# Making the low parts of fetched operands with an accumulating transfer

## The chip, the cores and the metric

The kernel runs on one core of a Trainium2 chip. The metric is the device time of one execution in microseconds (us). The engines of a core are named as in the profile: PE is TensorE (matrix products), with PEld for its weight loads; DVE is VectorE and ACT is ScalarE; POOL is GpSimd, and SP is SyncE, which here only issues transfers.

## The reference

One inference step of a transformer layer of width 2048, in fp32, over 512 prompt frames and 8 × 16 new frames, 640 tokens in all. Two groups of attention heads share one input projection; then come the output projection, a gated feed-forward block of 44 × 128 = 5632 columns and a last norm. The change touches the feed-forward block alone:

```python
def merge_and_ffn(x, oa, ob, norm_grp_a, norm_grp_b, w_out, norm_ffn, w_gate, w_up, w_down):
    o = jnp.concatenate([rmsnorm(oa, norm_grp_a), rmsnorm(ob, norm_grp_b)], axis=-1)
    x = x + o @ w_out
    h = rmsnorm(x, norm_ffn)
    return x + (jax.nn.silu(h @ w_gate) * (h @ w_up)) @ w_down
...
    y_prompt = rmsnorm(xp, norm_final)
```

## The kernel before, in words

**Two parts of a number.** An fp32 value goes to PE as a high part, rounded to the format fp32r, and a low part, the value minus the high part. `split` makes both: ACT writes the high part (L168), DVE subtracts it from the value (L169). `mm3` then issues three matmuls per tile: high weight by high operand (L177), high weight by low operand (L178), low weight by high operand (L179).

**Seven products for eight.** Matrices are cut into 2 × 2 blocks, and the four output blocks are built from seven products instead of eight. The tokens are cut into two halves of HT = 320. `quartet` loads four blocks of a weight matrix with SP (L874), forms sums of them on DVE (L887, L889) and on POOL (L891, which overwrites b11 and is needed by p5; L898, which overwrites b21 and is needed by p4), and multiplies in the order p1, p6, p7, p2, p5, p4, p3. Each product is emptied from its bank on ACT or DVE (L908). The operand sums that belong to product number `which` (0 to 6) are prepared once.

**Half 1** loops over 22 pairs of column blocks, for each over w_gate and w_up, K = 8 tiles per product. The gate goes through a Silu and two multiplications (L970 to L972), the product of gate and up is made on DVE (L976), and POOL forms the four operand sums that half 2 needs (L980 to L983). Three blocks of the pair as they are and the four sums, seven tiles in all, are stored by SP to `act_d` in DRAM, in four transfers (L984, and L986 three times).

**Half 2** walks 32 steps t. Step t adds to output blocks t mod 8 and t mod 8 + 8 the products over the five or six pairs that are active then (the table START says when a pair enters; it stays for eight steps). A pair's seven operands come back from `act_d` by `fetch`: SP loads a raw tile of 128 x 320 (L918), ACT writes its high part (L920), and DVE (where `which` is a multiple of 3) or POOL subtracts to give the low part (L921). The fetches for pairs that enter at step t + 1 are issued two products after the one that frees their space, in `fetch_waiting`. Blocks of x2 that a step adds to are loaded at L1010 and L1011. From step 24 on, squares of the finished blocks are also summed, on POOL (L248).

**The transition** is the last w_up quartet of half 1. As each of its products ends, `free(which)` releases the operands of half 1 and fetches those of the five pairs of step 0: pair loads of two tiles (L932), then `fetch` on each, the low part of the first of two on DVE and of the second on POOL. That makes 35 fetches, and the steps do 154 more.

**Order.** Each engine takes its instructions from one queue in order. The framework that builds the kernel lays the queues, so that the order on an engine isn't everywhere that of the text; it also adds the semaphore waits.

Of the kernel before, what the change touches and what calls it, by code (L numbers as in the profile page):

```python
# [7 lines left out]
AF = mybir.ActivationFunctionType  # L8
ALU = mybir.AluOpType
# [8 lines left out]
HT = 320  # L18
# [10 lines left out]
NPAIR = NFF // 2  # L29
# [4 lines left out]
def active(step):  # L34

    return [j for j in range(NPAIR) if (step - START[j]) % STEPS < 8]
# [5 lines left out]
def f(ap):  # L42
    return ap.bitcast(F32)


def halves(ap):
    return ap.rearrange("p (a b) -> p a b", a=2)


class Net:  # L50
# [20 lines left out]
    def add(self, queue, work):  # L71
        self.queues.setdefault(queue, []).append(work)
# [179 lines left out]
def sh(t, *shape):  # L252
    v = t[:, :int(np.prod(shape))]
    if len(shape) == 2:
        v = v.rearrange("p (a b) -> p a b", a=shape[0])
    elif len(shape) == 3:
        v = v.rearrange("p (a b c) -> p a b c", a=shape[0], b=shape[1])
    return v
# [11 lines left out]
def build(nc, tc, io, pools):  # L270
    n = Net(nc, tc, io, pools)
    dma = nc.sync.dma_start
# [12 lines left out]
    def dram(name, shape):  # L285
        return pools["dr"].tile(list(shape), F32, tag=name, name=name)
# [7 lines left out]
    def pack(t, k):  # L294
        v = r(sh(t, 2, k))
        return v[:, 0], v[:, 1]
# [476 lines left out]
    x2_d, act_d = dram("x2_d", (KT, P, TOK)), dram("act_d", (7, P, NPAIR, HT))  # L773
# [135 lines left out]
    prep = prepare([5, 6, 7], [7])  # L909
    lefts = [[None] * 7 for _ in range(NPAIR)]  # L910

    def fetch(j, which, raw=None, engine=nc.gpsimd):
        t, spare = n.get("S"), None
        if raw is None:
            if len(n.lists["S"]) > 3:
                spare = n.get("S")
            raw = n.scratch() if spare is None else spare[:, :HT]
            dma(out=raw, in_=act_d[which, :, j])  # L918
        hi, lo = hl = pack(t, HT)
        nc.scalar.activation(hi, raw, AF.Identity)  # L920
        engine.tensor_tensor(lo, raw, f(hi), ALU.subtract)  # L921
        if spare is not None:
            n.put("S", spare)
        lefts[j][which] = t, hl

    def free(which):
        n.put("S", *(h[which][0] for h in hs))
        ready = active(0)
        for j in ready[::2]:
            k = min(2, ready[-1] + 1 - j)  # L930
            raw = n.get("S")
            dma(out=sh(raw, k, HT), in_=act_d[which, :, j:j + k])  # L932
            for a in range(k):
                fetch(j + a, which, raw[:, a * HT:a * HT + HT], (nc.vector, nc.gpsimd)[a])
            n.put("S", raw)

    gate = None
    for i in range(NPAIR):
        for src in ("w_gate", "w_up"):
            blocks = [(2 * i, 0), (2 * i + 1, 0), (2 * i, 8), (2 * i + 1, 8)]  # L940
            load = lambda z: io[src][blocks[z][0], :, blocks[z][1]:blocks[z][1] + 8]
            y = n.get("S"), n.get("S")
            c11, c21, c12, c22 = y[0][:, :HT], y[0][:, HT:], y[1][:, :HT], y[1][:, HT:]
            start, end = i == 0 and src == "w_gate", i == NPAIR - 1 and src == "w_up"
            for step, bank in quartet(8, load, hs, (lambda w: next(prep)) if start else None, free if end else None):
                if step == "p1":
                    nc.scalar.activation(c11, bank, AF.Identity)
                elif step == "p6":
                    add(c12, c11, bank)
                elif step == "p7":  # L950
                    add(c21, c12, bank)
                elif step == "p5":
                    add(c22, c21, bank)
                    add(c12, c12, bank)
                elif step == "p2":
                    add(c11, c11, bank)
                elif step == "p4":
                    add(c21, c21, bank)
                elif step == "p3":
                    add(c12, c12, bank)  # L960
            if start:
                for _ in prep:
                    pass
                n.move("W", "H", 2)
                r_f = n.get("S")
                n.rstd(ssq, D, r_f)
                n.put("S", ssq)
            if src == "w_gate":
                for x in y:
                    nc.vector.tensor_tensor(x, x, r_f, ALU.mult)  # L970
                    nc.scalar.activation(x, x, AF.Silu)
                    nc.gpsimd.tensor_tensor(x, x, r_f, ALU.mult)  # L972
                gate = y
            else:
                for x, g in zip(y, gate):
                    nc.vector.tensor_tensor(x, x, g, ALU.mult)  # L976
                u, w = gate
                tt = nc.gpsimd.tensor_tensor
                s3, s1, s2, s4 = u[:, :HT], u[:, HT:], w[:, :HT], w[:, HT:]
                tt(s1, c21, c22, ALU.add)  # L980
                tt(s3, c21, c11, ALU.subtract)
                tt(s2, s1, c11, ALU.subtract)
                tt(s4, c12, s2, ALU.subtract)  # L983
                dma(out=act_d[0, :, i], in_=c11)  # L984
                for t, pick in ((w, slice(1, 7, 5)), (u, slice(2, 4)), (y[1], slice(4, 6))):
                    dma(out=act_d[pick, :, i].rearrange("w p c -> p w c"), in_=halves(t))  # L986
                n.put("S", *gate, *y)
    n.put("S", r_f)

# [3 lines left out]
    def fetch_waiting(left):  # L993
        while len(waiting) > left:
            for j, which in waiting.pop(0):
                fetch(j, which, engine=(nc.vector if which % 3 == 0 else nc.gpsimd))

    def step(t, part="all"):
        now = active(t)
# [3 lines left out]
        def after(which):  # L1003
            n.put("S", *(lefts[j][which][0] for j in now if j not in nxt))
            waiting.append([(j, which) for j in nxt if j not in now])
            fetch_waiting(2)
# [79 lines left out]
    for name in step(STEPS - 2, "late"):  # L1086
        if name == "p2":
            next(norm)
    fetch_waiting(0)
    squares(6, 0)  # L1090
    pass
# [98 lines left out]
```

## Time and profile before

| what | value |
|---|---|
| median of 3 runs | 2677.78 us (2677.6 to 2683.37) |
| the profiled execution | 2685.62 us, span 2683.8 us, mean granted clock 0.989 |
| PE, DVE, ACT, POOL busy | 2600.3, 1925.1, 1081.2, 789.5 us |
| bytes moved by transfers | 332.23 MB, mean 124 GB/s |
| half 1 ends, half 2 begins | about 2068 us into the span |

Busy time is that of an engine's compute instructions. SP's rows, marked SPq, are issues of transfers and their waits. A row of a timeline gives the start in us, the duration in us, engine, line, operation, the output's and inputs' names and the tile; in brackets stand the idle time before it and what ended it. In groups by line the columns are busy us and mean ns, then the idle time before and what ended it; in the table of waits: us in total, times, longest. W are weight tiles, S operand and sum tiles, `half` a separate buffer for raw tiles, and `at` and `dn` are the banks PE writes to.

### The profile page before, as it was taken

Reading aid. Unit: us, or ns where it says so; the run is one execution under the profiler, and the core shown is the slowest. Engines: PE = TensorE matmul, PEld = TensorE weight load, DVE = VectorE, ACT = ScalarE, POOL = GpSimd, SP = SyncE. Lnnn points to the kernel's source line nnn. Section 1 sums busy time; section 2 is a strip of 40 time slices with the busy share of each in tenths; the row PEclk is TensorE's granted clock in tenths of the full one; section 3 lists DMA queues with packets and bytes.
Section 4 is the critical chain, followed back from the end, with each engine's and each line's share of the span. In section 5 each row is a group of like instructions: output and inputs, shape, how many; then the busy total and the mean of one; then the engine's idle time right before and its main releaser. Section 6 shows DMA issues by size and latency. Waiting matters only on the chain.

```text
span 2683.8 us, 44823 instructions
## 1 busy us (share of the span) xinstructions
PE 2600.3 (97%) x17565; PEld 2540.1 (95%) x17565; DVE 1925.1 (72%) x2956; ACT 1081.2 (40%) x1759; POOL 789.5 (29%) x564
## 2 busy tenths in 40 slices
PE   7999999999999999999999999999999999999986
PEld 7999999899899999999999999999999899999986
DVE  7555566655866877667676667666678888888897
ACT  4333344434633643333333333333334444444443
POOL 3000000000302223333433433333335434344354
PEclk9999999999999999999999999999999999999998
DMA  5222223333655432332333333333325644444344
GB/s 162 89 72 89 96 66 105 119 120 130 214 188 194 152 123 96 109 117 97 120 104 112 118 104 106 116 106 105 121 96 174 216 132 127 130 133 129 108 114 139
DMA packets 154147, 332.23 MB, mean 124 GB/s; under 512 B 18064, under 2 KB 69264, under 8 KB 153936
## 3 DMA queue, kind: packets, MB, share of 16 engines
q1 hardware_dynamic: 153936, 329.38, 38.9%
q8 instruction: 138, 2.26, 0.4%
q14 instruction: 73, 0.60, 0.1%
HBM read 274.38 MB, written 54.20 MB: 122 GB/s over the span
## 4 chain that ended last, share of the span: by engine, by line
PE 84%; DVE 7%; DMA 3%; issue 3%; ACT 2%; POOL 0%; SPq 0%; DVEq 0%; ACTq 0%; POOLq 0%
PE dn L177 18%; PE dn L179 18%; PE dn L178 17%; PE at L177 9%; PE at L178 8%; PE at L179 8%; DVE W L169 2%; PE at L289 2%; PE at L367 1%; DVE S L908 1%; DMA W<-w_down 1%; DMA S<-act_d 1%; PE at L185 1%; PE at L184 1%; DVE S L1079 1%
## 5 line engine op out<-in xcount | busy, mean ns | idle before, releaser
L177 PE MATMUL dn<-S,W 128*128 128x320 f32 x3694 | 1164.0, 315 | 17.5 <-ACT S L920 7.1
L179 PE MATMUL dn<-S,W 128*128 128x320 f32 x3694 | 1149.6, 311 | 16.6 <-DVE W L169 16.5
L178 PE MATMUL dn<-S,W 128*128 128x320 f32 x3694 | 1148.3, 311 | 2.2 <-DVE S L173 1.1
L168 ACT ACTIVATE W<-W 128x1024 fp32r<-128x1024 f32 (+2 forms) x632 | 608.3, 964 | 1047.3 <-PE dn L178 524.7
L169 DVE TENSOR_TENSOR W<-W,W 128x1024 fp32r<-128x1024 f32 (+2 forms) x632 | 771.0, 1220 | 132.1 <-ACT W L168 128.3
L177 PEld LDWEIGHTS dn<-S,W 128*128 128x128 f32 x3694 | 698.7, 189 | 32.3 <-issue 9.5
L179 PEld LDWEIGHTS dn<-S,W 128*128 128x128 f32 x3694 | 698.4, 189 | 21.9 <-DVE W L169 21.2
L178 PEld LDWEIGHTS dn<-S,W 128*128 128x128 f32 x3694 | 699.0, 189 | 4.5 <-DVE S L173 1.4
L179 PE MATMUL at<-S,W 128*128 128x320 f32 x1594 | 494.0, 310 | 7.0 <-DVE W L169 6.9
L177 PE MATMUL at<-S,W 128*128 128x320 f32 x1594 | 493.4, 310 | 0.1
L178 PE MATMUL at<-S,W 128*128 128x320 f32 x1594 | 493.2, 309 | 0.0
L891 POOL TENSOR_TENSOR W<-W,W 128x1024 f32<-128x1024 f32 (+2 forms) x76 | 163.4, 2150 | 592.5 <-DVE W L169 523.0
L179 PEld LDWEIGHTS at<-S,W 128*128 128x128 f32 x1594 | 299.7, 188 | 9.9 <-DVE W L169 9.8
L177 PEld LDWEIGHTS at<-S,W 128*128 128x128 f32 x1594 | 299.8, 188 | 0.4 <-ACT W L168 0.4
L178 PEld LDWEIGHTS at<-S,W 128*128 128x128 f32 x1594 | 299.9, 188 | 0.0
L908 DVE TENSOR_TENSOR S<-S,dn 128x320 f32<-128x320 f32 x358 | 164.1, 481 | 95.9 <-PE dn L179 94.5
L887 DVE TENSOR_TENSOR W<-W,W 128x1024 f32<-128x1024 f32 (+2 forms) x76 | 133.7, 1759 | 100.3 <-DMA W<-w_up 51.3
L898 POOL TENSOR_TENSOR W<-W,W 128x1024 f32<-128x1024 f32 (+2 forms) x76 | 166.3, 2188 | 110.0 <-DVE W L169 104.6
L908 DVE TENSOR_TENSOR S<-S,at 128x320 f32<-128x320 f32 x262 | 123.2, 480 | 69.2 <-PE at L179 69.2
L248 POOL TENSOR_TENSOR S<-S,S 128x640 f32<-128x640 f32 x40 | 75.4, 1885 | 149.4 <-ACT S L247 148.6
L889 DVE TENSOR_TENSOR W<-W,W 128x1024 f32<-128x1024 f32 (+2 forms) x76 | 82.8, 1090 | 36.7 <-DMA W<-w_gate 24.8
L505 POOL MEMSET S<- 80x640 f32 x9 | 5.7, 629 | 309.9 <-PE at L185 185.8
(146 smaller groups left out, 2285.7 us busy)
## 6 DMA issues: line engine op xcount, KB each, us to landing
W<-w_gate SPq DMA_DIRECT2D x88, 512.0 KB
W<-w_up SPq DMA_DIRECT2D x88, 512.0 KB
W<-w_in SPq DMA_DIRECT2D x66, 512.0 KB
W<-w_down SPq DMA_DIRECT2D x64, 384.0 KB
W<-w_down SPq DMA_DIRECT2D x68, 320.0 KB
act_d<-S SPq DMA_DIRECT2D x66, 320.0 KB
half<-act_d SPq DMA_DIRECT2D x81, 160.0 KB
S<-act_d SPq DMA_DIRECT2D x80, 160.0 KB
```

Source lines behind the costliest of these rows:

```text
L168: self.nc.scalar.activation(hi, src, AF.Identity)
L169: self.nc.vector.tensor_tensor(lo, src, f(hi), ALU.subtract)
L177: mm(out, a[0], b[0], start=first, stop=False)
L178: mm(out, a[0], b[1], start=False, stop=False)
L179: mm(out, a[1], b[0], start=False, stop=last)
L248: (eng or nc.gpsimd).tensor_tensor(ssq, ssq, sq, ALU.add)
L289: nc.tensor.transpose(out, src, n.ident)
L887: nc.vector.tensor_tensor(b12[:, w], b12[:, w], b22[:, w], sub)
L889: nc.vector.tensor_tensor(s6[:, w], b11[:, w], b12[:, w], sub)
L891: nc.gpsimd.tensor_tensor(b11[:, w], b22[:, w], s6[:, w], sub)
L898: nc.gpsimd.tensor_tensor(b21[:, w], b21[:, w], s6[:, w], sub)
L908: add = lambda o, a, b: nc.vector.tensor_tensor(o, a, b, ALU.add)
```

## The change

In `fetch`, ACT writes the high part as before (now L921) and then, as a second activation with scale −1, the negated high part into the low part's tile (L922). A transfer issued by POOL reads the same 160 KB of `act_d` again and adds them onto that tile (L923), which gives value minus high part. The raw tile is no longer read by DVE or POOL. All 189 fetches go this way, those of `free` too, and the choice of an engine is gone. Besides, for the last pair of half 1 the four stores of operands to `act_d` are issued by POOL instead of SP.

```diff
-    def fetch(j, which, raw=None, engine=nc.gpsimd):
+    def fetch(j, which, raw=None):
...
         hi, lo = hl = pack(t, HT)
         nc.scalar.activation(hi, raw, AF.Identity)
-        engine.tensor_tensor(lo, raw, f(hi), ALU.subtract)
+        nc.scalar.activation(lo, f(hi), AF.Identity, scale=-1.0)
+        nc.gpsimd.dma_start(out=lo, in_=act_d[which, :, j], accum_op=ALU.add)
...
             for a in range(k):
-                fetch(j + a, which, raw[:, a * HT:a * HT + HT], (nc.vector, nc.gpsimd)[a])
+                fetch(j + a, which, raw[:, a * HT:a * HT + HT])
...
-                dma(out=act_d[0, :, i], in_=c11)
+                store = nc.gpsimd.dma_start if i == NPAIR - 1 else dma
+                store(out=act_d[0, :, i], in_=c11)
                 for t, pick in ((w, slice(1, 7, 5)), (u, slice(2, 4)), (y[1], slice(4, 6))):
-                    dma(out=act_d[pick, :, i].rearrange("w p c -> p w c"), in_=halves(t))
+                    store(out=act_d[pick, :, i].rearrange("w p c -> p w c"), in_=halves(t))
...
     def fetch_waiting(left):
         while len(waiting) > left:
             for j, which in waiting.pop(0):
-                fetch(j, which, engine=(nc.vector if which % 3 == 0 else nc.gpsimd))
+                fetch(j, which)
```

On ACT around the start of step 0, before (W_3138, W_3140 and W_3143 are the high parts of the first three weights of step 0; W_3138's stands five rows ahead of these):

```order
1137 L920 ACTIVATE S_3118_21229<-S_3117_21227 128x320
1138 L920 ACTIVATE S_3122_21263<-S_3121_21261 128x320
1139 L920 ACTIVATE S_3123_21266<-S_3121_21261 128x320
1140 L168 ACTIVATE W_3140_21331<-W_3137_21307 128x640
1141 L920 ACTIVATE S_3125_21271<-S_3124_21269 128x320
1142 L920 ACTIVATE S_3126_21274<-S_3124_21269 128x320
1143 L920 ACTIVATE S_3128_21279<-S_3127_21277 128x320
1144 L920 ACTIVATE S_3145_21371<-S_3146_21372 128x320
1145 L168 ACTIVATE W_3143_21352<-W_3134_21300 128x640
```

and now:

```order
1170 L922 ACTIVATE S_3123_21297<-S_3123_21297 128x320
1171 L921 ACTIVATE S_3125_21303<-S_3124_21301 128x320
1172 L921 ACTIVATE S_3126_21307<-S_3124_21301 128x320
1173 L922 ACTIVATE S_3125_21303<-S_3125_21303 128x320
1174 L922 ACTIVATE S_3126_21307<-S_3126_21307 128x320
1175 L921 ACTIVATE S_3128_21313<-S_3127_21311 128x320
1176 L168 ACTIVATE W_3138_21344<-W_3136_21339 128x640
1177 L922 ACTIVATE S_3128_21313<-S_3128_21313 128x320
1178 L168 ACTIVATE W_3140_21366<-W_3137_21342 128x640
1179 L168 ACTIVATE W_3143_21387<-W_3134_21335 128x640
1180 L921 ACTIVATE S_3145_21406<-S_3146_21407 128x320
```

The splits of W_3138, W_3140 and W_3143 stood among the high parts of fetched tiles; now they stand behind the 35 pairs of high part (L921) and negated high part (L922) that `free` makes, all but the last negated one.

On POOL at the same place, before (W_3136 is b11 of step 0, W_3147 its b21; S_3021 and S_3022 hold operand sums of the last pair):

```order
387 L921 TENSOR_TENSOR S_3116_21224<-S_3114_21219,S_3116_21224 128x320
388 L891 TENSOR_TENSOR W_3136_21304<-W_3135_21302,W_3137_21307 128x640
389 L921 TENSOR_TENSOR S_3123_21266<-S_3121_21261,S_3123_21266 128x320
390 L921 TENSOR_TENSOR S_3126_21274<-S_3124_21269,S_3126_21274 128x320
391 L981 TENSOR_TENSOR S_3021_20682<-S_3047_20912 128x320
392 L980 TENSOR_TENSOR S_3021_20682<-S_3047_20912,S_3048_20913 128x320
393 L982 TENSOR_TENSOR S_3022_20683<-S_3021_20682,S_3047_20912 128x320
394 L921 TENSOR_TENSOR S_3151_21400<-S_3152_21401,S_3151_21400 128x320
395 L983 TENSOR_TENSOR S_3022_20683<-S_3048_20913,S_3022_20683 128x320
396 L921 TENSOR_TENSOR S_3155_21426<-S_3156_21427,S_3155_21426 128x320
397 L921 TENSOR_TENSOR S_3160_21453<-S_3161_21454,S_3160_21453 128x320
398 L898 TENSOR_TENSOR W_3147_21378<-W_3147_21378,W_3137_21307 128x640
```

and now:

```order
411 L923 DMA S_3126_21307<-act_d 128x320
412 L923 DMA S_3128_21313<-act_d 128x320
413 L891 TENSOR_TENSOR W_3136_21339<-W_3135_21337,W_3137_21342 128x640
414 L923 DMA S_3145_21406<-act_d 128x320
415 L982 TENSOR_TENSOR S_3021_20682<-S_3047_20912,S_3048_20913 128x320
416 L989 DMA act_d<-S_3048_20913 128x2x320
417 L984 TENSOR_TENSOR S_3022_20683<-S_3021_20682,S_3047_20912 128x320
418 L989 DMA act_d<-S_3021_20682 128x2x320
419 L985 TENSOR_TENSOR S_3022_20683<-S_3048_20913,S_3022_20683 128x320
420 L923 DMA S_3151_21436<-act_d 128x320
421 L989 DMA act_d<-S_3022_20683 128x2x320
422 L898 TENSOR_TENSOR W_3147_21414<-W_3147_21414,W_3137_21342 128x640
```

Between the last gate's multiplication (L974 now, two rows: numbers 373 and 374) and the first row here stand 33 accumulating transfers, one store (L987), one L898 (W_3086) and one L983. So ahead of L891 of W_3136 are the 35 low parts that `free` fetches and a store, and between it and L898 of W_3147 are three stores and two low parts more, with the sums of the last pair.

On SP at the same place, before:

```order
690 L874 DMA W_3147_21378<-w_down 128x640
691 L984 DMA act_d<-S_3047_20912 128x320
692 L918 DMA S_3152_21401<-act_d 128x320
693 L918 DMA S_3156_21427<-act_d 128x320
694 L918 DMA S_3161_21454<-act_d 128x320
695 L918 DMA S_3165_21479<-act_d 128x320
696 L1010 DMA S_3166_21484<-x_d 128x640
697 L986 DMA act_d<-S_3021_20682 128x2x320
698 L986 DMA act_d<-S_3022_20683 128x2x320
699 L986 DMA act_d<-S_3048_20913 128x2x320
700 L1011 DMA S_3167_21485<-x_d 128x640
701 L874 DMA W_3170_21490<-w_down 128x640
```

and now:

```order
687 L874 DMA W_3147_21414<-w_down 128x640
688 L1013 DMA S_3129_21328<-x_d 128x640
689 L1014 DMA S_3130_21329<-x_d 128x640
690 L919 DMA S_3146_21407<-act_d 128x320
691 L919 DMA S_3152_21437<-act_d 128x320
692 L919 DMA S_3156_21464<-act_d 128x320
693 L919 DMA S_3161_21492<-act_d 128x320
694 L874 DMA W_3170_21530<-w_down 128x640
695 L919 DMA S_3165_21518<-act_d 128x320
696 L1013 DMA S_3166_21524<-x_d 128x640
697 L1014 DMA S_3167_21525<-x_d 128x640
```

The four stores of the last pair are gone from SP's queue, and the loads of fetched tiles (L919 now) and weights follow each other without them.

## The prediction

> **What bounds the kernel now.** I read the page first: which engine fills the span.
>
> ```profile
> span 2683.8 us, 44823 instructions
> PE 2600.3 (97%) x17565; PEld 2540.1 (95%) x17565; DVE 1925.1 (72%) x2956; ACT 1081.2 (40%) x1759; POOL 789.5 (29%) x564
> ```
>
> TensorE (PE) is busy for 97% of the span, so a change on the other engines can win only where PE idles. The table of stages (window, its length, then busy time of PE, PEld, DVE, ACT and POOL, granted clock, DMA share, GB/s) shows where that is, in the part with fetches:
>
> ```profile
> 2050.00:2078.00 28.00, 25.25 (x158) 24.38 (x157) 27.16 (x32) 18.26 (x40) 20.25 (x14) 0.94 0.77 252
> 2078.00:2100.00 22.00, 16.70 (x98) 16.08 (x96) 17.77 (x24) 7.98 (x16) 13.44 (x12) 0.84 0.66 215
> 2160.00:2500.00 340.00, 336.35 (x2293) 335.86 (x2291) 288.28 (x393) 146.88 (x229) 138.77 (x91) 1.00 0.47 132
> 2500.00:2640.00 140.00, 124.79 (x810) 119.48 (x808) 126.42 (x182) 63.90 (x108) 71.07 (x46) 0.99 0.40 113
> ```
>
> PE idles 2.8 + 5.3 us around the transition from half 1 to half 2, 3.7 us in the long middle and 15.2 us in the last eight steps. All that this change can win is there. The late stage has DVE at 126.4 of 140 us, and the waits of PE there are:
>
> ```profile
> PE at L179 <- DVE W L169: 6.9, 7, 1.6
> PE dn L179 <- DVE W L169: 4.2, 4, 2.4
> PE dn L177 <- DVE S L908: 3.6, 3, 2.3
> ```
>
> All 14.7 us of them name DVE: late there is the split of a weight (L169) or the emptying of a bank (L908). At the transition the timelines of PE say
>
> ```profile
> 2070.30 0.42 PE L179 MATMUL dn<-S,W 128*128 128x320 f32 x1 [1.82 <-DVE W L169]
> 2083.55 0.60 PE L177 MATMUL dn<-S,W 128*128 128x320 f32 x1 [4.77 <-ACT S L920]
> ...
> 2092.29 0.31 PE L177 MATMUL dn<-S,W 128*128 128x320 f32 x1
> ...
> 2094.81 0.42 PE L179 MATMUL at<-S,W 128*128 128x320 f32 x1
> ...
> 2100.61 0.42 PE L179 MATMUL dn<-S,W 128*128 128x320 f32 x1 [1.14 <-DVE W L169]
> 2103.88 0.39 PE L177 MATMUL dn<-S,W 128*128 128x320 f32 x1 [1.10 <-DVE S L908]
> ```
>
> The third row is the first matmul of p5 of step 0, the fourth the first of p4 that reads a weight's low part.
>
> **The change on the late DVE.** It takes 87 L921 subtractions off DVE and 102 off POOL (52 + 35, 56 + 46):
>
> ```profile
> L921 POOL TENSOR_TENSOR S<-S,S x56: 875/1140/1899, 2048.6 to 2644.6; 128x320 fp32r<-128x320 f32 x56
> L921 DVE TENSOR_TENSOR S<-S,S x52: 475/483/2700, 2048.4 to 2641.7; 128x320 fp32r<-128x320 f32 x52
> L921 POOL TENSOR_TENSOR S<-half,S x46: 872/1357/1705, 2199.2 to 2489.5; 128x320 fp32r<-128x320 f32 x46
> L921 DVE TENSOR_TENSOR S<-half,S x35: 477/479/1693, 2201.4 to 2493.9; 128x320 fp32r<-128x320 f32 x35
> ```
>
> What that is worth between 2500 and 2640 comes from the groups by shape (busy us, mean ns), with the quickest split beside them:
>
> ```profile
> L169 DVE TENSOR_TENSOR W<-W,W 128x640 fp32r<-128x640 f32 x50 | 55.7, 1114 | 1.8 <-ACT W L168 1.5
> L887 DVE TENSOR_TENSOR W<-W,W 128x640 f32<-128x640 f32 x8 | 13.4, 1674 | 5.9 <-DMA W<-w_down 5.9
> L921 DVE TENSOR_TENSOR S<-S,S 128x320 fp32r<-128x320 f32 x14 | 9.9, 708 | 2.8 <-ACT S L920 2.8
> ...
> L921 POOL TENSOR_TENSOR S<-S,S 128x320 fp32r<-128x320 f32 x19 | 23.3, 1233 | 28.2 <-ACT S L920 25.3 <-PE at L178 2.8
> ...
> 2519.18 0.81 DVE L169 TENSOR_TENSOR W<-W,W 128x640 fp32r<-128x640 f32 x1
> ```
>
> DVE loses 9.9 us of its own L921. Beyond that, the same split takes 0.81 us or, on the mean, 1.114: something stretches it. If that is POOL at work beside it, the stretch over L169 is 50 × 0.30 = 15.2 us and over L887 8 × (1.674 − 0.81) = 6.9, together 22 us against POOL's 71.07 us of busy time. L921's part of POOL is 23.3/71.07 = 33%, so 7.2 us of stretch go with it, and DVE gets 9.9 + 7.2 = 17 us in a stage where PE waits 15.2 us for it. Not all of that arrives: each step also waits for its weights, which SyncE (SP) cannot load before a buffer is free:
>
> ```profile
> SPq L874 <- POOL W L898: 15.7, 7, 4.2
> ```
>
> and then the load itself has to land, a piece of about 3 us in the late chain of waits:
>
> ```profile
> 2531.33 3.01 DMA W<-w_down
> ```
>
> I take 60% of PE's idle time, **−9 us**; bounds −15 (all of it) and −3 (only a third of L921's own 9.9, as when loads set the pace). The page "SBUF — State Buffer" of the Trainium skill, section "Who interferes with whom", says that a DVE instruction with two operands in SBUF contends with a GpSimd instruction that reads SBUF, not with one that only writes it. By that rule the accumulating issues, which read no tile, leave the 7.2 us free; the stretched L169 rows agree with its first half, and no run here shows the second. Without it DVE would get 9.9 us, and the late term would be about −6.
>
> Middle stage: 3.7 us of idle, of which I take **−2.5**; bounds −3.7 and 0.
>
> **The new work on ACT.** 189 more ACTIVATEs. Price, from the transition:
>
> ```profile
> 2056.17 1.19 ACT L920 ACTIVATE S<-S 128x320 fp32r<-128x320 f32 x3 [3.25 <-DMA S<-act_d]
> 2057.27 1.04 ACT L168 ACTIVATE W<-W 128x1024 fp32r<-128x1024 f32 x1
> ...
> 2061.62 3.15 ACT L920 ACTIVATE S<-S 128x320 fp32r<-128x320 f32 x8
> ...
> 2070.04 0.72 ACT L168 ACTIVATE W<-W 128x640 fp32r<-128x640 f32 x1
> ...
> 2075.19 1.17 ACT L920 ACTIVATE S<-S 128x320 fp32r<-128x320 f32 x3
> ```
>
> 3.15/8 = 0.39 us each, so 74 us more on an engine with 40% load. In the steps idle ACT covers it (63.9 of 140 us busy late; the 33 pairs fetched there, 14 + 19 by L921's rows, are 13 us at 0.39). Uncovered it would be those 13 us. At the transition the first split of a w_down weight (L168 at 2070.04) now stands behind the hi and lo of all 35 pairs that free fetches. Of these, 33 lie between 2051.2 and the last row shown: 66 × 0.39 = 26 us, with three L168 of 128x1024 at 1.04 and a bank's copy of 0.4 between them, so it starts near 2081. p1 of step 0 then begins near 2082.8 (0.72 for L168, some 0.8 for L169). PE issues a matmul every 0.147 us (336.35 us for 2293 in the middle stage), so a product of five pairs, 15 matmuls, takes 2.2, and four of them (p1, p6, p7, p2) lead to p5 at 2091.6, where before had it at 2092.29: one wait stands in for the stalls of 1.82 and 4.77. I take **0 us**, if POOL isn't later; if ACT's wait of 3.25 us at 2056 stays in full, +3.
>
> **The new work on POOL.** 189 accumulating issues and four stores, 193 in all, none of which has a row, since before issues everything from SP:
>
> ```profile
> 2072.76 0.38 SPq L918 DMA_DIRECT2D S<-act_d  x1
> ```
>
> SP issues a load of this tile in 0.38 us; POOL's quickest operation on the tile took 0.875, its slowest 1.90 (first row of L921). My bounds for the price x of one issue on POOL are 0.38 and 1.90. I take **x = 0.9**, the middle one, since POOL must do something for each of the 128 rows. The page "DMA: Bandwidth & Descriptors" of the Trainium skill, section "Latency and other measured facts", gives about 1 us to the first byte for a transfer issued from GpSimd, which nothing here shows; by x = 1.0 the sum below would be 4 us higher.
>
> At the transition these issues stand in one queue with L898, L981, L891 and the sums of the last pair:
>
> ```profile
> 2052.11 1.83 POOL L921 TENSOR_TENSOR S<-S,S 128x320 fp32r<-128x320 f32 x1
> 2053.90 2.66 POOL L898 TENSOR_TENSOR W<-W,W 128x1024 f32<-128x1024 f32 x1
> ...
> 2076.64 1.76 POOL L891 TENSOR_TENSOR W<-W,W 128x640 f32<-128x640 f32 x1 [2.77 <-DVE W L169]
> 2080.83 1.10 POOL L981 TENSOR_TENSOR S<-S 128x320 f32<-128x320 f32 x1
> 2084.62 1.39 POOL L980 TENSOR_TENSOR S<-S,S 128x320 f32<-128x320 f32 x1 [2.70 <-DVE S L976]
> 2086.09 1.33 POOL L982 TENSOR_TENSOR S<-S,S 128x320 f32<-128x320 f32 x1
> 2088.47 0.87 POOL L983 TENSOR_TENSOR S<-S,S 128x320 f32<-128x320 f32 x1
> 2091.56 1.56 POOL L898 TENSOR_TENSOR W<-W,W 128x640 f32<-128x640 f32 x1
> ```
>
> From 2052.11, where POOL had finished L972 of the last gate: 36 issues × 0.9 = 32.4, L898 2.66, the sum of L981 1.10, L891 1.76: done at 2090.0, in time for p5. Then five more issues 4.5, the sums 1.39 + 1.33 + 0.87, L898 1.56: done at 2099.7. The split of that weight (L168 0.72, L169 0.81) ends at 2101.2, and p4's L179, at 2094.81 before, comes **+6.4 us** late. Queued behind it on PE is p3 and all of step 1; in return the waits of 1.14 and 1.10 us at 2100 and 2103 find their work done, **−2.2**. Each 0.1 us on x is 41 × 0.1 = 4.1 us here, so x = 0.38 ends in no loss at all (PE then follows ACT: −2), x = 1.90 in +47.
>
> **The added transfers.** 189 × 160 KB = 31 MB more. The late engines are 40% busy, so a load of w_down (3.01 us above) waits a little more: 0.2 us × 8 steps = **+1.6**; bounds 0 and +5.
>
> **The sum**: −9 − 2.5 + 6.4 − 2.2 + 1.6 = −5.7 us, for an execution that took 2685.62 us when profiled (span 2683.8): 2679.9. That execution is 7.8 us above the median of the runs, 2677.78; for the median the forecast is **2672.1 us**. Lowest by the bounds: −15 − 3.7 − 2 + 0 = −20.7, 2657; highest: +47 − 2.2 − 3 + 5 = +47, 2725.
>
> **Rivals.** (a) *The relief doesn't reach PE.* In the last steps the loads of weights set the pace, behind L898 (15.7 us of SP's waits above) and 3 us of landing, and the late term is −3: −5.7 + 6 = +0.3, 2678.1. For it: both DVE and loads alternate in the late chain. Against it: PE's waits name DVE alone.
>
> (b) *POOL's queue at the transition decides (slower).* With x = 1.3 (the mean of POOL's own L921 was 1.2 late), the 41 issues cost 16.4 us more than I took: p4 of step 0 comes 22.8 us late, the sum is −5.7 + 16.4 = +10.7, 2688.5. It decides from x = 0.9 + 5.7/41 = 1.04. For it: such an issue is made by a program, none was measured, and L891 and L898 can't overtake the queue. Against it: the quickest POOL rows are at 0.87.
>
> (c) *The transfers are the bound at the transition (slower).* The engines are 77% busy at 252 GB/s there, so full at 327. 35 lows of 163,840 bytes are 5.73 MB: 17.5 us of full engines, and 35 if an addition, which also reads its target, takes twice as long. Free are 28 × 0.23 + 22 × 0.34 = 13.9 us. The excess, 3.6 to 21, on the mean 12.3, delays weights and lows alike: −5.7 + 12.3 = +6.6, 2684.4. Against it: the loads of pairs for free end by 2078, with a third of the engines idle after them.
>
> (d) *The edit isn't what it says*: the additions could also be forced one behind the other. Eight at a time by the semaphores, with 3 us of landing, are 0.4 us each, under x; I give it nothing.
>
> **How the numbers follow.** No change and a difference can be told apart here at about 0.2%, 5.4 us. Forecast 0.40, (a) 0.22, (b) 0.27, (c) 0.11. That is faster 0.40, same 0.22, slower 0.38. The range holds 2657 (the low bounds) to 2700: (b) up to x = 1.58, which is past its middle; above it lies about a tenth, below the low end as much. The forecast's own range is 2657 to 2676.
>
> **What would show it.** An accumulating issue on POOL should take 0.9 us; over 1.04 gives (b), with L891 and L898 of step 0 late in POOL's timeline and PE waiting for them near 2092 to 2115. The first split of step 0 should come near 2081. In the last eight steps PE's idle should fall from 15.2 to about 6 us and L169's mean from 1.114 towards 1.0; if that mean falls and the idle stays, it is (a). DMA share near 1.0 between 2050 and 2100, and matmuls that read lows (L178) waiting on transfers, would be (c). A long wait of SP for POOL's L921 should be gone. The forecast is wrong if the late idle stays, or if anything behind POOL's queue comes later than p4 of step 0.

## The result

The changed kernel takes 2710.46 us (median of 4 runs, 2706.91 to 2714.53), the kernel before 2677.71 us beside it: a ratio of 1.0118, 95% interval 1.0097 to 1.0139. It is slower by some 32 us, where I had forecast 5.7 us faster. The profiled execution has a span of 2710.8 us at a mean granted clock of 0.984.

The stages of the changed kernel, with the same columns as before (window, length, busy time of PE, PEld, DVE, ACT, POOL, granted clock, DMA share, GB/s; x counts the instructions):

```profile
2050.00:2078.00 28.00, 17.51 (x96) 16.38 (x95) 10.98 (x10) 21.01 (x54) 21.31 (x23) 0.76 1.10 272
2078.00:2100.00 22.00, 16.32 (x104) 14.89 (x102) 7.89 (x12) 12.55 (x29) 13.88 (x18) 0.99 1.14 274
2100.00:2160.00 60.00, 45.22 (x240) 43.18 (x241) 29.49 (x45) 24.25 (x49) 27.61 (x29) 0.81 0.81 212
2160.00:2500.00 340.00, 333.16 (x2244) 331.90 (x2243) 257.89 (x350) 184.42 (x318) 145.50 (x129) 0.99 0.74 175
2500.00:2640.00 140.00, 134.46 (x899) 131.51 (x898) 114.98 (x167) 78.42 (x139) 71.67 (x59) 1.00 0.70 161
```

The third window was, in the kernel before:

```profile
2100.00:2160.00 60.00, 56.95 (x379) 55.57 (x380) 52.96 (x77) 27.32 (x49) 25.16 (x19) 1.00 0.59 180
```

The late stage is as hoped: PE idles 5.5 of 140 us instead of 15.2. (The two windows don't hold quite the same steps, since the changed kernel is more than 30 us late there; step for step the gain is 7 us, in the table below.) The loss is at the transition, where PE idles 10.5 + 5.7 + 14.8 us between 2050 and 2160, and where the DMA share has gone from 0.77 to 1.10 while the rate only rose from 252 to 272 GB/s. (A share above 1 is possible, since the time of packets overlaps.)

PE's timeline there shows waits that the kernel before doesn't have:

```profile
2069.01 0.63 PE L177 MATMUL dn<-S,W 128*128 128x320 f32 x1 [9.44 <-ACT W L168]
...
2101.14 0.63 PE L177 MATMUL dn<-S,W 128*128 128x320 f32 x1 [4.51 <-ACT W L168]
...
2111.16 0.63 PE L177 MATMUL at<-S,W 128*128 128x320 f32 x1 [4.64 <-ACT W L168]
...
2112.45 0.47 PE L177 MATMUL at<-S,W 128*128 128x320 f32 x1
2112.72 0.47 PE L178 MATMUL at<-S,W 128*128 128x320 f32 x1
...
2117.49 0.31 PE L178 MATMUL dn<-S,W 128*128 128x320 f32 x1
2117.64 0.31 PE L179 MATMUL dn<-S,W 128*128 128x320 f32 x1
...
2122.92 0.39 PE L177 MATMUL dn<-S,W 128*128 128x320 f32 x1 [4.53 <-DVE S L908]
```

The rows with a wait are p5 of the last w_up quartet, still in half 1, then p5 and p4 of step 0, and p1 of step 1. The four rows without one show a second loss: for some 5 us behind such a wait PE starts a matmul only every 0.27 us, and then every 0.15 again; the granted clock of that window is 0.81 where it was 1.00. From p5 of the quartet to the start of step 2 the slow pace costs 15 us against the full one, where it cost 6 before. So of the 31 us lost by then, some 9 are no waits, but PE running slowly behind them.

POOL's timeline from the first of these waits on:

```profile
2070.74 0.86 POOL L923 DMA_DIRECT2D S<-act_d  x1 [0.87 <-DMA S<-act_d]
2072.44 0.86 POOL L923 DMA_DIRECT2D S<-act_d  x1 [0.84 <-DMA S<-act_d]
...
2097.91 0.85 POOL L923 DMA_DIRECT2D S<-act_d  x1 [0.81 <-issue]
2098.47 1.85 POOL L891 TENSOR_TENSOR W<-W,W 128x640 f32<-128x640 f32 x1
...
2106.33 2.10 POOL L898 TENSOR_TENSOR W<-W,W 128x640 f32<-128x640 f32 x1
```

The row of an issue is 0.86 us long, but it isn't POOL's time in full: where nothing holds POOL up, the next instruction starts 0.54 to 0.56 us after the issue's start, as L891 does at 2098.47. In this stretch, though, the issues start 0.9 to 1.7 us apart, 1.5 on the mean, because POOL waits for transfers to land: by the landing times of the trace, each of its 22 transfers from 2065.96 to 2097.91 is issued 0.50 to 0.60 us after the eighth before it has landed, and POOL never has more than eight under way. L891 of step 0 ends at 2100.3, where I had 2090.0, and L898 at 2108.4, where I had 2099.7.

For a comparison free of windows I set the n-th matmul of the two feed-forward halves against the n-th of the other trace. Below is how much later (us) the same matmul starts than in the kernel before, counted from p1 of the last w_up quartet, for the change and for the variants of the next section:

```
first of          before  change  free   steps   act    neg    plain  small  late
                                  old    old     only   dve
p5, last w_up     2060.7   +9.6   +0.0   +9.4   +0.6   +0.0   +6.9   +6.0   +0.0
p3, last w_up     2068.0  +13.9   +0.3  +13.8  +12.4   +1.5   +9.3   +8.7   +0.0
step 0, p1        2075.2  +12.1   +0.3  +11.9   +8.8  +12.9   +7.3   +6.8   +0.0
step 0, p5        2092.3  +10.1   +0.5  +14.0   +2.0  +12.5   -1.0   +0.1   +0.5
step 0, p4        2094.5  +18.0   +0.5  +16.5   +2.8  +18.4   +6.8   +1.9   +0.5
step 1, p1        2099.0  +25.2   +0.4  +23.2   +6.7  +20.5   +9.3   +2.5   +0.3
step 2            2117.4  +30.8   +3.6  +20.1  +11.5  +24.4   +8.0   +3.7   +0.3
step 9            2234.7  +35.6   +8.1  +17.5  +15.7  +30.1  +10.0   +0.4   -2.4
step 24           2511.9  +35.6   +8.4  +17.5  +15.7  +30.1  +10.0   +0.4   -2.4
step 26           2544.8  +36.7  +10.5  +17.1  +16.8  +31.1   +9.7   +0.5   -1.5
last matmul       2660.8  +29.5   +3.4  +17.3   +8.3  +22.5   -0.4   -9.6   -9.8
```

These are single executions; where nothing was changed ahead of a row, as in "late" before step 24, they differ by up to 2.4 us. The change loses 31 us up to step 2, another 6 up to step 26, and wins 7 after that. Between steps 9 and 24 nothing is lost or won in the change: there PE has hardly any idle time in the kernel before, and the transfers, though they raise the DMA share from 0.47 to 0.74 (between 2160 and 2500 us), don't hold it up.

### The profile page after: what moved, and what is told of

The parts are those of the page before. It is cut to its first block, busy times and chain, and to the rows that moved or that the text cites. A ratio compares the mean times of both kernels' runs of the same rounds, so it can differ in the third digit from the quotient of the medians.

```text
span 2710.8 us, 45073 instructions
## 1 busy us (share of the span) xinstructions
PE 2609.0 (96%) x17565; PEld 2546.4 (94%) x17565; DVE 1856.5 (68%) x2869; ACT 1158.1 (43%) x1948; POOL 820.8 (30%) x655
## 5 line engine op out<-in xcount | busy, mean ns | idle before, releaser
L179 PE MATMUL dn<-S,W 128*128 128x320 f32 x3694 | 1153.1, 312 | 21.0 <-DVE W L169 20.6
L168 ACT ACTIVATE W<-W 128x1024 fp32r<-128x1024 f32 (+2 forms) x632 | 607.2, 963 | 980.7 <-PE dn L178 510.0
L169 DVE TENSOR_TENSOR W<-W,W 128x1024 fp32r<-128x1024 f32 (+2 forms) x632 | 755.7, 1196 | 180.6 <-ACT W L168 175.5
L179 PEld LDWEIGHTS dn<-S,W 128*128 128x128 f32 x3694 | 701.0, 190 | 27.3 <-DVE W L169 26.8
L179 PE MATMUL at<-S,W 128*128 128x320 f32 x1594 | 495.6, 311 | 4.2 <-DVE W L169 4.0
L891 POOL TENSOR_TENSOR W<-W,W 128x1024 f32<-128x1024 f32 (+2 forms) x76 | 167.1, 2199 | 569.5 <-DVE W L169 511.2
L179 PEld LDWEIGHTS at<-S,W 128*128 128x128 f32 x1594 | 300.5, 189 | 8.5 <-DVE W L169 8.2
L908 DVE TENSOR_TENSOR S<-S,dn 128x320 f32<-128x320 f32 x358 | 164.1, 482 | 108.5 <-PE dn L179 101.5
L923 POOL DMA_DIRECT2D S<-act_d x189 | 167.5, 943 | 205.1 <-ACT S L922 154.8
L898 POOL TENSOR_TENSOR W<-W,W 128x1024 f32<-128x1024 f32 (+2 forms) x76 | 167.4, 2202 | 107.6 <-DVE W L169 103.0
L908 DVE TENSOR_TENSOR S<-S,at 128x320 f32<-128x320 f32 x262 | 123.3, 480 | 77.8 <-PE at L179 77.6
L248 POOL TENSOR_TENSOR S<-S,S 128x640 f32<-128x640 f32 x40 | 74.7, 1869 | 148.9 <-ACT S L247 148.1
```

The source lines that it names most:

```text
L168: self.nc.scalar.activation(hi, src, AF.Identity)
L169: self.nc.vector.tensor_tensor(lo, src, f(hi), ALU.subtract)
L179: mm(out, a[1], b[0], start=False, stop=last)
L248: (eng or nc.gpsimd).tensor_tensor(ssq, ssq, sq, ALU.add)
L891: nc.gpsimd.tensor_tensor(b11[:, w], b22[:, w], s6[:, w], sub)
L898: nc.gpsimd.tensor_tensor(b21[:, w], b21[:, w], s6[:, w], sub)
```

## The experiments

There are two theories for the transition. **T1**: ACT's doubled work there stands ahead of the splits that PE waits for. **T2**: the accumulating transfers fill the DMA engines, and all that goes through them comes late. A third, **T3**, is for the steps: the same transfers cost there too.

**Undo the transition alone** ("free old"): `free` makes its low parts with DVE and POOL again.

```diff
-    def fetch(j, which, raw=None):
+    def fetch(j, which, raw=None, engine=None):
...
-        nc.scalar.activation(lo, f(hi), AF.Identity, scale=-1.0)
-        nc.gpsimd.dma_start(out=lo, in_=act_d[which, :, j], accum_op=ALU.add)
+        if engine is not None:
+            engine.tensor_tensor(lo, raw, f(hi), ALU.subtract)
+        else:
+            nc.scalar.activation(lo, f(hi), AF.Identity, scale=-1.0)
+            nc.gpsimd.dma_start(out=lo, in_=act_d[which, :, j], accum_op=ALU.add)
...
-                fetch(j + a, which, raw[:, a * HT:a * HT + HT])
+                fetch(j + a, which, raw[:, a * HT:a * HT + HT], (nc.vector, nc.gpsimd)[a])
```

> The 35 fetches of the transition are made as in the kernel before (DVE and GpSimd subtract); the 154 of the steps, and the last pair's stores, stay as changed. Theory T1 (the splits of the last w_up quartet stand behind ACT's doubled work at the transition) and T2 (the accumulating transfers fill the DMA engines there) agree: the 34 us lost between the last w_up quartet and step 8 are gone, and the 6 us won from step 25 on remain: -6 us against before, about 2672 us, within 3 us. Rival T3 (the accumulating transfers of the steps cost too, since loads of weights land later): no gain or a loss, +0 to +6 us, 2678 to 2684.

Measured: ratio 1.0028 (1.0016 to 1.0040), +7.5 us. The big loss is gone, but so is the gain, which is T3, a little above its range. In the table the variant loses 10 us between step 0 and step 26, most of them by step 9, before it wins 7. It is a miss for the common expectation of T1 and T2, which had no price for the steps.

**Undo the steps alone** ("steps old"): only `free` accumulates. `fetch` is that of "free old", and now the steps name an engine.

```diff
             for j, which in waiting.pop(0):
-                fetch(j, which)
+                fetch(j, which, engine=(nc.vector if which % 3 == 0 else nc.gpsimd))
```

> The reverse: only the 35 fetches of the transition accumulate; the 154 of the steps are made as before. T1 and T2: the loss of the transition stays, the late gain of 6 us is gone: +25 to +34 us, about 2707 us. T3: with fewer transfers from step 0 on, the part of the loss that comes after p5 of step 0 (some 20 us) goes, and +10 to +14 us remain, about 2690 us.

Measured: 1.0073 (1.0059 to 1.0087), +19.5 us, between the two expectations. It loses 23 us up to step 1 and gets 6 of them back by step 9; after step 26 it wins nothing. So the late gain belongs to the accumulating fetches of the steps, and isn't just time lost earlier that comes back. The two halves, 0.28% and 0.73%, make 1.01% of the 1.18%.

**ACT's part without transfers** ("act only"): in `free` ACT writes both parts, and DVE or POOL adds the raw tile. `free` names an engine as in "free old"; the cut shows `fetch` alone, here and in the next run.

```diff
-        nc.scalar.activation(lo, f(hi), AF.Identity, scale=-1.0)
-        nc.gpsimd.dma_start(out=lo, in_=act_d[which, :, j], accum_op=ALU.add)
+        if engine is not None:
+            nc.scalar.activation(lo, f(hi), AF.Identity, scale=-1.0)
+            engine.tensor_tensor(lo, raw, f(lo), ALU.add)
+        else:
+            nc.scalar.activation(lo, f(hi), AF.Identity, scale=-1.0)
+            nc.gpsimd.dma_start(out=lo, in_=act_d[which, :, j], accum_op=ALU.add)
```

> In the 35 fetches of the transition ACT writes the high part and the negated high part as in the change, but DVE and GpSimd add the raw tile to it, as many operations on them as before, and no accumulating transfer. Steps and stores as changed. T1: p5 of the last w_up quartet still starts about 9 us late and the first split of step 0 some 10 us late; the total is 5 to 12 us above the variant with the old transition, about 2680 us. T2: within 3 us of that variant, about 2673 us.

Measured: 1.0049 (1.0036 to 1.0063), 2.1 thousandths or 5.6 us above "free old", though the two intervals just overlap. T1 is real in the trace, and small: PE is 12.4 us late at p3 of the quartet, but only 2.0 at p5 of step 0, since the kernel before itself loses time between the two, with waits (7.5 us, of which 1.2 remain) and with slow matmuls behind them (4.4 us, of which 0.3 remain).

**Transfers without ACT's part** ("neg dve"): in `free` DVE writes the negated high part.

```diff
-        nc.scalar.activation(lo, f(hi), AF.Identity, scale=-1.0)
+        if engine is not None:
+            nc.vector.tensor_scalar(lo, f(hi), -1.0, None, ALU.mult)
+        else:
+            nc.scalar.activation(lo, f(hi), AF.Identity, scale=-1.0)
         nc.gpsimd.dma_start(out=lo, in_=act_d[which, :, j], accum_op=ALU.add)
```

> In the 35 fetches of the transition DVE writes the negated high part, so that ACT has no more to do there than in the kernel before; the accumulating transfers stay. Steps and stores as changed. T1: p5 of the last w_up quartet is on time, and of the 34 us lost some 14 to 20 are gone, about 2690 us. T2: the transfers are as many, DMA share about 1.1 at the transition, and the total stays within 5 us of the changed kernel, 2705 to 2712 us.

Measured: 1.0088 (1.0071 to 1.0105), +23.6 us: 8 us better than the change, 16 us worse than "free old", and so between the two expectations. p5 of the quartet is on time, but the wait only moves to p1 of step 0 (12.9 us late), and p4 is as late as in the change. Most of the loss stays with the transfers, T2, unless DVE's 35 new operations cost as much, which this run doesn't tell. And a transfer is several things: a place in POOL's queue, bytes, and an addition.

**Bytes without the addition** ("plain"). This kernel leaves the addition out, so that the raw tile overwrites the negated high part; only its time is of use here.

```diff
-        nc.gpsimd.dma_start(out=lo, in_=act_d[which, :, j], accum_op=ALU.add)
+        nc.gpsimd.dma_start(out=lo, in_=act_d[which, :, j])
```

> The changed kernel with the addition left out of its 189 transfers: GpSimd's transfer overwrites the negated high part with the raw tile, so the low parts are wrong by the whole high part, and every queue holds the same rows. T2 in its sharp form (an adding transfer takes the DMA engines about twice as long per byte as a plain one): DMA share at the transition falls from 1.1 below 1.0, a third to a half of the loss goes, about 2695 us. If a plain transfer from GpSimd loads the engines as much, the time stays within 4 us of the changed kernel, about 2710 us.

Measured: 0.9998 (0.9989 to 1.0008). The whole loss is gone, not a third of it, with the same queues and the same 31 MB. The share of the DMA engines did not fall below 1; what changed is the rate:

```profile
2050.00:2078.00 28.00, 19.46 (x117) 18.54 (x116) 8.38 (x12) 26.20 (x66) 18.91 (x32) 0.88 1.19 368
2078.00:2100.00 22.00, 14.38 (x90) 13.76 (x90) 11.56 (x15) 11.63 (x27) 13.99 (x20) 0.84 1.14 375
```

368 and 375 GB/s, against 272 and 274 in the change. The queues' table (packets, MB, share of the engines) prices one transfer. The change:

```profile
q0 software_dynamic: 27504, 32.12, 7.5%
```

and "plain":

```profile
q0 software_dynamic: 27504, 32.12, 4.8%
```

Without the four stores (0.1% in the run that has only them), 7.4% of 2710.8 us over 189 transfers is 1.06 us of all 16 engines for one of 160 KB that adds, and 4.7% of 2679.8 is 0.67 for one that doesn't. (That is the time of their packets. It isn't due to full engines: in runs with 35 adding transfers alone it is 1.00 at the transition, from 1.4% with the stores in "steps old", and 1.14 us in the late steps, from 1.5% in the run "late" below.) SP's transfers in the kernel before, with the row

```profile
q1 hardware_dynamic: 153936, 329.38, 38.9%
```

come to 0.52 us per 160 KB. One thing else differs: the row of POOL's issue is shorter too. In the change

```profile
L923 POOL DMA_DIRECT2D S<-act_d x189: 850/860/2428, 2049.7 to 2676.6; - x189
DMA to landing us min/median/max: 3.3/4.9/12.0
```

and in "plain"

```profile
L923 POOL DMA_DIRECT2D S<-act_d x189: 528/531/715, 2047.6 to 2644.7; - x189
DMA to landing us min/median/max: 2.4/3.9/8.6
```

so this run alone doesn't tell POOL's queue from the engines. (The next instruction starts 0.52 us after such an issue at the soonest, against 0.54 in the change, so that the rows differ more than POOL's time.)

**The addition without most of the bytes** ("small"). This kernel adds 40 of 320 columns and leaves the rest of each low part out.

```diff
-        nc.gpsimd.dma_start(out=lo, in_=act_d[which, :, j], accum_op=ALU.add)
+        nc.gpsimd.dma_start(out=lo[:, :40], in_=act_d[which, :, j, :40], accum_op=ALU.add)
```

> The changed kernel with transfers of 40 of the 320 columns: an eighth of the bytes, the rest of each low part stays the negated high part, and order, ACT's and GpSimd's instructions are the same. T2 (traffic): the weights land in time again, what remains is ACT's order at the transition (+6 us) and the late gain (-7 us): 2676 to 2684 us. T1 (order and work on ACT and GpSimd): at least half of the loss stays, 2695 us or more.

Measured: 0.9966 (0.9952 to 0.9979), −9.1 us, faster than either theory had it. POOL's issue is as long as in the change,

```profile
L923 POOL DMA_DIRECT2D S<-act_d x189: 847/866/4352, 2045.8 to 2633.8; - x189
DMA to landing us min/median/max: 2.3/3.7/9.0
```

and POOL is busy for all of the transition; together with ACT's order that comes to 3.7 us by step 2:

```profile
2050.00:2100.00 50.00, 38.10 (x232) 35.83 (x230) 26.88 (x31) 40.34 (x99) 50.00 (x56) 0.93 1.03 281
```

So the issues themselves are not the cause, nor is ACT's order beyond a few us. It takes the bytes and the addition together: the transfers that add, at full size. Where POOL's queue holds PE up in the change, it is by the waits for their landing, which takes up to 12.0 us there and up to 9.0 here. The DMA share is 1.03 in this run too, so that a share of 1 alone doesn't mean a loss. And the 189 transfers still take 2.3% of the engines without the stores, 0.32 us each, a third and not an eighth of the full ones.

**Only the late fetches** ("late"): the kernel before, with accumulation where DVE is the bound.

```diff
-        t, spare = n.get("S"), None
+        again, (t, spare) = raw is None, (n.get("S"), None)
...
-        engine.tensor_tensor(lo, raw, f(hi), ALU.subtract)
+        if again and START[j] >= 25:
+            nc.scalar.activation(lo, f(hi), AF.Identity, scale=-1.0)
+            nc.gpsimd.dma_start(out=lo, in_=act_d[which, :, j], accum_op=ALU.add)
+        else:
+            engine.tensor_tensor(lo, raw, f(hi), ALU.subtract)
```

> The kernel before, with accumulating low parts only for the pairs that enter at steps 25 to 31 (35 of the 189 fetches); transition, the other steps and the stores as before. If the late relief of DVE is real and needs none of the rest: the 7 us that steps 26 to 31 won in the changed kernel, less some 2 us around steps 24 and 25: -5 us, about 2674 us, ratio 0.998. If the late gain was only the return of time lost earlier: no change.

Measured: 0.9962 (0.9949 to 0.9974), and when run again:

> The 35 late fetches accumulate, as in the run of that name, for comparison on one chip with the two others: ratio 0.996 again, -10 us.

0.9971 (0.9961 to 0.9982), 2671.31 us beside 2679.45. This version beats the kernel before by 8 to 10 us, more than the 5 expected, and 8 of them come from step 26 on.

**Only the stores**: the last pair's four stores on POOL, the rest as before (the edit is that of the change's diff).

> The kernel before with only the last pair's four stores issued by GpSimd. All theories: four issues of 0.9 us on GpSimd between L891 and L898 of step 0, which GpSimd did 1.4 us before p4 needed it: p4 up to 2 us late, total 0 to +2 us, 2678 to 2680 us.

Measured: 0.9997 (0.9988 to 1.0007). The stores cost nothing that can be seen.

**What of the late fetches wins?** First only those of DVE (15 of 35) accumulate; against "late":

```diff
-        if again and START[j] >= 25:
+        if again and START[j] >= 25 and which % 3 == 0:
```

> The kernel before, with accumulating low parts only for the products that DVE subtracted (which a multiple of 3) of the pairs that enter at steps 25 to 31: 15 of the 189 fetches; GpSimd subtracts the other 20 as before. If the late gain comes from DVE's own 13 to 15 subtractions (9.4 us): most of it stays, -6 to -10 us. If it needs GpSimd's subtractions gone too (stretched rows of DVE): less than half, -2 to -4 us.

Measured: 0.9989 (0.9980 to 0.9997), −3 us. Then all 35 are subtracted on POOL, with no transfer; against the kernel before:

```diff
-                fetch(j, which, engine=(nc.vector if which % 3 == 0 else nc.gpsimd))
+                fetch(j, which, engine=(nc.vector if which % 3 == 0 and START[j] < 25 else nc.gpsimd))
```

> The kernel before, with the low parts of the same 35 late fetches all subtracted by GpSimd, none on DVE, and no accumulating transfer. If DVE's own subtractions are the cost: -4 to -8 us, without any transfer. If GpSimd's reads beside DVE are the cost: 15 subtractions more on GpSimd take back what DVE gives up, 0 to +4 us.

Measured: 1.0007 (0.9998 to 1.0015): no gain. So freeing DVE of its own subtractions is the smaller part, and POOL's must go too. The groups of DVE over steps 24 to 30, in one execution of each, show why (busy us, mean ns). In the kernel before:

```profile
L169 DVE TENSOR_TENSOR W<-W,W 128x640 fp32r<-128x640 f32 x48 | 54.1, 1126 | 1.7 <-ACT W L168 1.3
...
L908 DVE TENSOR_TENSOR S<-S,S 128x320 f32<-128x320 f32 x21 | 13.8, 708 | 0.0
```

With DVE's 15 alone accumulating, POOL still subtracting:

```profile
L169 DVE TENSOR_TENSOR W<-W,W 128x640 fp32r<-128x640 f32 x48 | 59.6, 1244 | 4.6 <-ACT W L168 4.2
...
L908 DVE TENSOR_TENSOR S<-S,S 128x320 f32<-128x320 f32 x21 | 12.4, 641 | 0.0
```

"Late", all 35:

```profile
L169 DVE TENSOR_TENSOR W<-W,W 128x640 fp32r<-128x640 f32 x48 | 53.7, 1118 | 11.4 <-ACT W L168 11.0
...
L908 DVE TENSOR_TENSOR S<-S,S 128x320 f32<-128x320 f32 x21 | 9.0, 480 | 0.0
```

As long as POOL subtracts, DVE's other operations stretch, and the split takes back 5.5 of the 9.4 us that were freed. With POOL's subtractions replaced by issues, these two rows lose 9.3 us more.

## Why the prediction was wrong

**The step that failed is the term "the added transfers".** I had it at +1.6 us, bounds 0 and +5, by pricing 31 MB as a slight delay of eight loads in the late stage. Measured it is about 41 us: the ratio of the change, 1.0118, less that of "small", 0.9966, is 1.5% of 2679 us. Some 9 us of that (0.9998 − 0.9966) come with the bytes as plain transfers, and 32 us (1.0118 − 0.9998) with the addition, which also lengthens the row of POOL's issue by 0.33 us. I asked of the late engines, 40% busy, and not of the transition (77%) nor of steps 0 to 9, where "free old" loses some 8 us. The term had no place for two things: POOL, which stands still until transfers land, and PE, for which I counted 0.147 us per matmul throughout and which runs slowly behind each long wait (some 9 of the 31 us up to step 2).

**Rival (c) named the mechanism** and I gave it 0.11 and +12.3 us above the forecast. Its price per transfer was right at its upper end: twice the plain 17.5 us for 35 transfers is 1.0 us each, and 1.06 was measured. Two things made it dearer. It counted the excess of the engines' work between 2050 and 2100 alone, where the steps add theirs (+10 us up to step 26). And the delay reached all that passes through the engines, weights and raw tiles too. In the changed kernel the waits of ACT and DVE for transfers grew, from 2040 us to the end:

```profile
ACT S L921 <- DMA S<-act_d: 76.7, 47, 6.0
...
DVE W L887 <- DMA W<-w_down: 52.1, 32, 6.0
```

In the kernel before they were:

```profile
ACT S L920 <- DMA S<-act_d: 56.0, 36, 3.8
...
DVE W L887 <- DMA W<-w_down: 26.4, 28, 2.0
```

That an adding transfer reads its target, and so takes twice as long, was my reason for the doubling; the price is shown, the reason isn't.

**What I dismissed in (d) was part of it.** The 0.4 us that I worked out there for each issue, from eight at a time and 3 us of landing, used a landing time of a quiet stage. With only the transition accumulating the median to landing is

```profile
DMA to landing us min/median/max: 5.6/11.3/12.4
```

and 11.3/8 is 1.4 us per issue, over x. The timeline names different waits for POOL there, but the landing times settle it: each issue follows the landing of the eighth before it by 0.50 to 0.60 us, and the issues stand 1.5 us apart.

**Price x: right as the length of a row, too high as time in POOL's queue.** The row of an issue is 0.86 us long (median), where I took 0.9, but the next instruction can start after 0.54. The page "DMA: Bandwidth & Descriptors" of the Trainium skill gives about 1 us to the first byte of a transfer from GpSimd in "Latency and other measured facts"; the row of an issue doesn't measure a first byte, and no row here shows one. Rival (b), which decides from 1.04 us per issue, fell as a price. Its signs are there all the same, L891 and L898 late and PE waiting behind them; they come from the waits for landing.

**The transition without traffic: right in sum, and that is luck.** I had +6.4 − 2.2 = +4.2 us; "small" is 3.7 us late at step 2. But p4's first low part (L179) is 2.5 us late there and not 6.4, as the issues pass in less than 0.9 us, and the 2.2 us don't come back by step 2. And one step was missed: I followed ACT's queue only up to the first split of step 0 (2081 forecast, 2085.2 measured in the change) and overlooked the splits of the last w_up quartet in the same queue. The second row here is the split for which p5 of that quartet waited 9.44 us, behind some eight us of such pairs with no gap over 0.7 us:

```profile
2067.56 0.45 ACT L921 ACTIVATE S<-S 128x320 fp32r<-128x320 f32 x1
2067.92 1.04 ACT L168 ACTIVATE W<-W 128x1024 fp32r<-128x1024 f32 x1
```

In "small" this costs 8.7 us up to p3 of the quartet. It is gone by p5 of step 0 (+0.1), because the stalls of 1.82 and 4.77 us of before, and the slow matmuls behind them, lie right there; I had used the stalls for p5 of step 0.

**The late term: right in size.** The forecast was −9 us; the change wins 7.2 from step 26 on, "late" 8.3. DVE's busy time over steps 24 to 30 fell from 118.54 to 101.34 us, the 17 us that I had worked out. How it splits was off: L169's mean stayed at 1.11 us and the relief came in L908 on sums, 708 to 480 ns; "late" against "only DVE's 15" shows that POOL's part counts. That agrees with the Trainium skill, "SBUF — State Buffer", section "Who interferes with whom": a subtraction on POOL reads SBUF, and DVE's operations with two operands there stretch; with issues in place of the subtractions the sums are at 480 ns. It isn't shown that an issue touches nothing, since L169 stays long beside L898, L891 and L248. The gap to the full 15 us has a new wait in it: DVE's L169 waits 11.0 us for ACT's L168 there ("late"), where it waited 1.3.

**The middle term: unclear.** The forecast was −2.5 us. Some 2.4 us up to step 9 are gone in the runs that leave that stage as it was, too ("late" in the table), so that they belong to the one execution of before that was profiled.

## What to carry to other kernels

Replacing an operation by an accumulating transfer moves its cost to the DMA engines, and there an addition was half as dear again as a plain transfer issued the same way and twice a plain load from SP. So price it by the share of the engines in each stage through which it passes, not by bytes and not by the issue: it won where the engines were 40% busy and DVE was the bound, changed nothing where they were 47% busy and PE was the bound (steps 9 to 24), and lost where they were 59 to 77% busy. And when a queue's new work is counted up to the instruction one has in mind, every earlier instruction behind the same work has to be looked at too.

## What had not been expected of the hardware

With the engines full, the core's rate was 272 to 274 GB/s with the adding transfers in the mix, and 368 to 375 with plain ones from the same queue. The row of an issue on POOL followed the addition (0.86 against 0.53 us) and not the bytes (0.87 us for 40 of 320 columns), but the next instruction could start 0.54 us after an adding issue and 0.52 after a plain one. Behind a wait of 4.6 us PE started matmuls every 0.27 us for some 5 us, and then every 0.15. In the late stage the share rose from 0.40 to 0.70 and the rate from 113 to 161 GB/s, and PE idled less than before.
